# RWKV-7 time mixing: the recurrence's small products in column tiles of 32, outputs between the state products

## Chip, cores and metric

The kernel runs on one core of one Trainium2 chip. The metric is device time in microseconds (us); lower is better. A time is the median of several executions; one further execution is taken by the hardware profiler, and all rows below come from it.

## What is computed

The reference is one residual layer: RMS norm, an RWKV-7 mixer, an output projection. x is 2048 x 1024 float32, with 16 heads of 64. After projections that give r, k, v, a gate g, a decay w and a rate a for each token, each head runs a recurrence over the 2048 tokens:

```python
def step(S, inp):
    r_t, w_t, k_t, v_t, kk_t, a_t = inp
    sa = einsum('bhvk,bhk->bhv', S, -kk_t)
    S = S * w_t[:, :, None, :] + sa[..., None] * (kk_t * a_t)[:, :, None, :] + v_t[..., None] * k_t[:, :, None, :]
    y_t = einsum('bhvk,bhk->bhv', S, r_t)
    return S, y_t
```

Its output y is normalised per head and token (group norm), a bonus sum(r k r_k) v is added, the result is multiplied by silu(g) and by w_out, and x is added.

## The kernel before

**Chunks, halves, blocks.** The recurrence is computed in 64 chunks of 32 tokens (`L = 32`). The 16 heads are 8 pairs; a *wave* w is four pairs, and `h` is the head of a pair. So a chunk is two *halves*, wave 0 and wave 1, and each half issues these blocks of small products on TensorE, 64 columns of data each, in float32 (one product is two instructions in the trace, so 8 products are 16 instructions):

- **S**, `r_state` (line 245): weights `st[:, h, pair]` (128 rows x 64 columns) against the tile `x`, whose 128 rows hold the 32 tokens' values (`kv` rows), 32 rows for the results of U (`bu` rows) and the 64 x 64 state. The results of head h go to 64 PSUM rows of `bank[w]`: 32 rows for U, 32 rows with the state's part of the output. ScalarE copies the former to `misc` (line 254, two copies).
- **U**, `r_u` (line 256): the inverted 32 x 32 matrix of the chunk times these rows, 32 rows deep, in tiles of 32 x 32. ScalarE copies the result into the `bu` rows of `x` (line 265).
- **D**, `r_d` (line 267): 128 x 64 weights `dk` against `x`, into `bank[3]`; VectorE multiplies by the decay and writes the state rows of the next chunk's `x` (line 281; in the rows it has the helper's line 51).
- **Y**, `r_y` (line 284): adds to S's output rows what U's result contributes, 32 rows deep, in tiles of 32 x 32; ScalarE copies the sum to the output tile `y` (line 297).

S of a wave needs the state that D and VectorE wrote in the chunk before; U needs S's copies; D and Y need U's copies. The two waves alternate: while one waits, the other's blocks run. `chunk` (line 299) writes the order out by hand.

**Two loops.** Chunks 0 to 8 run inside the last part of the projections (`last`, `fill_last`, lines 1059 to 1171). Chunks 9 to 63 run in a loop of their own (line 1236), and three queues of other work are issued between their blocks:

- `work`: for each 128 tokens (four chunks, y tile t) a *tail* of items (`tail`, line 339), queued after chunk 4t + 4: squares on ScalarE, sums and a Newton reciprocal root on VectorE and GpSimd, normalise, gate weight and bonus on VectorE (`norm` and `bonus`, lines 407 to 414, four parts), transposes on TensorE (line 424, two groups of four, into one PSUM buffer `tps`), `shift`, `gating` and `rest` (lines 433 to 443) on VectorE with a cast on ScalarE (line 439). Chunks 12 to 40 also queue ten items of the inversions for the last two blocks of tokens (`inversion`, line 486). Each item has a nominal cost; `None` items are markers.
- `dense`: the 48 products 128 x 128 x 512 of a tail's output projection (`mm`, line 449), queued by the tail's last item.
- `evacs`: their stores.

`background(us)` (line 1193) sets its budget to `min(left + us, us)`, then issues items from `evacs` or `work` until the next one costs more than is left, or is a marker; it issues one item at least. `fill(n)` (line 328) issues dense products. `BG = 1.6` and `F = (2, 4)` are on line 29.

In a chunk, `background(BG)` is called after S of each wave (as `state`), and by `after` (line 1230) after U of each wave, there with `fill(6)`. Each engine runs its instructions in the order in which they are issued here (`manual_schedule`, line 1215).

The y tiles of this loop have three buffers. `new_y` calls `more_y` (line 1208): for t above 5 it calls `background(1)` until the second transposes of tail t - 3 have been issued.

```python
        def more_y(t):
            while t > 5 and t - 3 not in turned:
                background(1)
            return yp.tile([P, 2, NP, N], F32, name=f"y{t}", tag="y", bufs=3)
```

After the loop, line 1252 issues what is left: `while work or dense or evacs: background(2); fill(6)`.

Of the kernel before, what the change touches and what calls it, by code (L numbers as in the profile page):

```python
# [24 lines left out]
L = 32  # L25
TB = 256
NC = TB // L
NORM_EPS = 1e-6
F, BG, EV, EV0, GWE, BNE, LOW, SLOW, FAST, INV, INVC = (2, 4), 1.6, (0, 0, 0), (0, 0, 0), 0, 0, 36, 0.7, 1.3, (8, 10), 0.5
LIM = 1.0  # L30
INL = (0, 0, 3, 3, 3, 0, 0, 0)
INA, INB = (0, 0, 0, 4, 3, 3, 3, 1), (0, 0, 4, 2, 2, 2, 0, 1)
# [7 lines left out]
def rwkv7_kernel(ctx, tc, a, T):  # L40
    nc = tc.nc
# [164 lines left out]
    kv = lambda h: slice(64 * h, 64 * h + L)  # L206
    bu = lambda h: slice(64 * h + L, 64 * h + 2 * L)
    ca, cr = slice(0, L), slice(L, 2 * L)
    half = lambda h: slice(64 * h, 64 * h + 64)
    stat, dk, xs = [], [], []  # L210
# [14 lines left out]

    pls, bns, ys, misc, bank, evs, more = {}, {}, {}, [], [None] * 4, list(EV0), [None]
    first = [0]
    live = lambda w: misc[0][:, 256 * w : 256 * w + 256].rearrange("p (q n) -> p q n", q=4)

    def new_y(t):  # L230
        ys[t] = more[0](t)
# [10 lines left out]
    def ev(i, h):  # L242
        return nc.vector.tensor_copy if h < evs[i] else nc.scalar.copy

    def r_state(ch, w):
        st, x, y = stat[ch % len(stat)], xs[ch % len(xs)], bank[w][:, ch % 2]
        for p in range(4):
            for h in range(2):
                nc.tensor.matmul(y[half(h), p], st[:, h, 4 * w + p], x[:, h, 4 * w + p], start=(p == 0), stop=(p == 3),  # L249
                                 tile_position=(0, 64 * h))  # L250
        gs = live(w)
        with urgent():
            for h in range(2):
                nc.scalar.copy(gs[bu(h)], y[kv(h)])  # L254

    def r_u(ch, w):
        st, x, gs = stat[ch % len(stat)], xs[ch % len(xs)], live(w)
        for p in range(4):
            for h in range(2):
                rb = bu(h)  # L260
                nc.tensor.matmul(bank[2][rb, p], st[rb, h, 4 * w + p, ca], gs[rb, p], start=True, stop=True,
                                 tile_position=(rb.start, rb.start))
        with urgent():
            for h in range(2):
                ev(0, h)(x[bu(h), h, 4 * w : 4 * w + 4], bank[2][bu(h)])

    def r_d(ch, w):
        if ch + 1 == NCH:
            return
        d, x = dk[ch % len(dk)], xs[ch % len(xs)]  # L270
        dp = bank[3]
        for p in range(4):
            for h in range(2):
                nc.tensor.matmul(dp[half(1 - h), p], d[:, h, 4 * w + p], x[:, h, 4 * w + p], start=True, stop=True,  # L274
                                 tile_position=(0, 64 * (1 - h)))
        g, c = divmod(ch, NC)
        with urgent():
            for h in range(2):

                H = half(1 - h)  # L280
                tt(xs[(ch + 1) % len(xs)][H, h, 4 * w : 4 * w + 4], dp[H],
                   pls[g][H, c, 4 * w : 4 * w + 4, None].broadcast_to([64, 4, N]), mul)

    def r_y(ch, w):
        st, x, c = stat[ch % len(stat)], xs[ch % len(xs)], ch % 4
        for p in range(4):
            for h in range(2):
                rb = bu(h)
                nc.tensor.matmul(bank[w][rb, ch % 2, p], st[rb, h, 4 * w + p, cr], x[rb, h, 4 * w + p], start=False,  # L289
                                 stop=(p == 3), skip_group_check=True, tile_position=(rb.start, rb.start))  # L290
        t = ch // 4
        if c == 0 and w == 0:
            new_y(t)
        with urgent():
            for h in range(2):
                o = 64 * h + L * (c % 2)
                ev(2, h)(ys[t][o : o + L, c // 2, 4 * w : 4 * w + 4], bank[w][bu(h), ch % 2])

    def chunk(ch, state, fill):

        g, c = divmod(ch, NC)
        if c == 2 and g + 1 < NB:
            load_g(g + 1)
        r_state(ch, 0)
        state()
        if ch != first[0]:
            r_d(ch - 1, 1)
        fill(0)
        if ch != first[0]:
            r_y(ch - 1, 1)  # L310
        if ch + 2 < NCH:
            load_v(ch + 2)
        if ch + 3 < NCH:
            load_c(ch + 3)
        r_u(ch, 0)
        fill(1)
        r_state(ch, 1)
        state()
        r_d(ch, 0)
        fill(2)  # L320
        r_y(ch, 0)
        r_u(ch, 1)
        fill(3)

    dense, evacs, turned, served, al = deque(), deque(), set(), [0.0, 0.0], {}
    eng = lambda i: nc.gpsimd if i else nc.vector

    def fill(n):

        served[0] = min(served[0], 6) + n * (FAST if len(dense) > 2 * LOW else 1 if len(dense) > LOW else SLOW)  # L330
        while served[0] > 0 and dense:
            dense.popleft()[0]()
            served[0] -= 1
# [170 lines left out]
    with ExitStack() as p0:  # L504
# [37 lines left out]
        with ExitStack() as pa:  # L542
# [48 lines left out]
            for b in range(NB):  # L591
                (mvh, mvl), (mgh, mgl) = mixa, mixb
                lps = pps.tile([P, TB], F32, name=f"lps{b}", tag="lps", bufs=1)
                for ct in range(NCT):
                    h, dx, xt = make_h(b, ct, bc, "a")
# [3 lines left out]
                    for i in range(2):  # L599
                        tok = slice(1 - i, TB + 1 - i)  # L600
                        for k, (x, y) in enumerate(((0, hh), (0, hl), (1, hh))):
                            nc.tensor.matmul(lps, wls[i][x][:, ct], y[:, tok], start=(ct == 0 and i == 0 and k == 0),
                                             stop=(ct == NCT - 1 and i == 1 and k == 2))
# [51 lines left out]
        with ExitStack() as pb:  # L655
# [234 lines left out]
            def preload():  # L890

                misc.append(wtile("misc", [P, D], F32))
                aux = wtile("aux", [P, D], F32)
                al["gw"] = aux[:, 0:512].rearrange("p (h n) -> p h n", n=N)
                al["aux"] = iter(aux[:, x : x + 16].rearrange("p (k h) -> p k h", k=2) for x in range(512, 1024, 16))
                nc.sync.dma_start(al["gw"], a["gn_w"].rearrange("p (h n) -> p h n", n=N))
                stat.extend(wtile(f"stat{i}", [P, 2, NP, 64], F32) for i in range(4))
                dk.extend(wtile(f"dk{i}", [P, 2, NP, 64], F32) for i in range(4))
                xs.extend(wtile(f"x{i}", [P, 2, NP, N], F32) for i in range(3))
                y0 = [wtile(f"y0{t}", [P, 2, NP, N], F32) for t in range(3)]  # L900
                more[0] = lambda t: y0[t]
                for h in range(2):
                    H = half(1 - h)
                    nc.gpsimd.memset(xs[0][H, h], 0.0)

                    for x in dk:
                        nc.gpsimd.tensor_copy(x[H, h], ident[H, None, H].broadcast_to([64, NP, N]))
                load_v(0)
                load_c(0)
# [263 lines left out]
    with ExitStack() as p1:  # L1173
# [19 lines left out]
        def background(us):  # L1193

            served[1] = min(served[1] + us, us)
            fresh = True
            while evacs or work:
                u, fn = (evacs or work)[0]
                if not fresh and (u is None or u > served[1]):
                    break  # L1200
                (evacs or work).popleft()
                if u is None:
                    continue
                fresh = False
                fn()
                served[1] -= u
# [8 lines left out]
        with tc.manual_schedule(engines=MANUAL):  # L1215
            work.extend((0.7, lambda q=q: wo_split(NP - 1, q)) for q in range(2))
            for x in tail(1):
                work.extend(x)
            z = c1.tile([P, L, L], F32, name="z_")
            tm = c1.tile([P, 4 * N], F32, name="tm_")  # L1220
            inv = deque()
            for g in (NB - 2, NB - 1):
                load, *cols = inversion(g, z, lambda: tm)
                inv.extend([(0, load)] + [(None, None), (0, lambda: None)] * 4)
                inv.extend((INVC, x) for x in cols)
            inv_g = inv[L + 6][1]

            inv_last = inv[-1][1]

            def after(i):  # L1230

                if i % 2:
                    background(BG)
                    fill(sum(F))

            for ch in range(NC + 1, NCH):
                chunk(ch, lambda: background(BG), after)
                if ch % 4 == 0 and ch > NC:
                    for x in tail(ch // 4 - 1):
                        work.extend(x)  # L1240
                    for i in range(INV[1] if ch >= INV[0] else 0):
                        if inv:
                            work.append(inv.popleft())
                if ch == NCH - 2 * NC - 4:
                    assert len(inv) <= L - 1 and not any(x[1] is inv_g for x in work)
                if ch == NCH - NC - 4:
                    assert not inv and not any(x[1] is inv_last for x in work)
            r_d(NCH - 1, 1)
            r_y(NCH - 1, 1)
            for x in tail(NCH // 4 - 1):  # L1250
                work.extend(x)
            while work or dense or evacs:
                background(2)
                fill(6)
# [52 lines left out]
```

## Time and profile before

| | us |
|---|---|
| median of 3 runs (1638.33 to 1648.4) | 1640.22 |
| the profiled execution | 1642.18 |
| its span, first to last instruction | 1640.4 |

| engine | busy us | share of the span |
|---|---|---|
| TensorE, products (PE) | 1529.5 | 93% |
| TensorE, weight loads (PEld) | 1325.5 | 81% |
| VectorE (DVE) | 1192.3 | 73% |
| ScalarE (ACT) | 835.3 | 51% |
| GpSimd (POOL) | 359.8 | 22% |

The mean granted TensorE clock is 0.978 of full speed. Products are pipelined: one small product is shown with some 0.22 us, though the next starts long before its end, so a busy TensorE still has waits inside. In a row, the time in brackets is what the engine was idle before it, with what released it.

### The profile page before, as it was taken

How to read it: one execution, taken by the hardware profiler on the slowest of the kernel's cores; microseconds unless marked ns; L12 is line 12 of the kernel's file. 1: busy time of each engine (PE TensorE's matmuls, PEld its weight loads, DVE VectorE, ACT ScalarE, POOL GpSimd, SP SyncE). 2: the span in 40 equal slices, each digit the busy share in tenths (PEclk: the TensorE clock that was granted, in tenths of full speed). 3: DMA queues.
4: the chain of work that ended last, by engine and by line, in shares of the span. 5: the costliest groups of instructions: out<-in, count | busy, mean ns of one | idle time of the engine just before them, and what ended most of it. 6: DMA issues, size and time to landing. Idle time of an engine off the chain costs nothing. (4 is left out here: it accounts for less than half of the span.)

```text
span 1640.4 us, 45953 instructions
## 1 busy us (share of the span) xinstructions
PE 1529.5 (93%) x17776; PEld 1325.5 (81%) x17776; DVE 1192.3 (73%) x2844; ACT 835.3 (51%) x2126; POOL 359.8 (22%) x727
## 2 busy tenths in 40 slices
PE   3799999999989999999999999898899999999998
PEld 2589889999888888889888988777677788777776
DVE  7976776668646469797988888568568867776654
ACT  5653332233346454554545454577566666666551
POOL 4500000000002132322323232412233222323221
PEclk9899999999999999999999999799999999999999
DMA  5773433334474565666675766778866687677632
GB/s 181 225 259 126 145 117 112 127 129 155 131 233 115 124 145 139 141 155 146 156 152 153 154 160 153 216 190 236 214 186 182 176 200 207 177 182 198 177 108 81
DMA packets 445739, 269.14 MB, mean 164 GB/s; under 512 B 302768, under 2 KB 386096, under 8 KB 445520
## 3 DMA queue, kind: packets, MB, share of 16 engines
q1 hardware_dynamic: 444176, 261.67, 58.9%
q10 hardware_dynamic: 1344, 4.52, 1.0%
q8 instruction: 141, 2.31, 0.6%
q14 instruction: 78, 0.64, 0.1%
HBM read 158.74 MB, written 111.54 MB: 165 GB/s over the span
## 5 line engine op out<-in xcount | busy, mean ns | idle before, releaser
L540 PE MATMUL gps<-mixbh,wgh 128*128 128x256 f32 x512 | 147.0, 287 | 6.2 <-ACT vo L635 6.2
L540 PE MATMUL gps<-mixbl,wgh 128*128 128x256 f32 x512 | 146.5, 286 | 0.0
L540 PE MATMUL gps<-mixbh,wgl 128*128 128x256 f32 x512 | 146.4, 286 | 0.0
L254 ACT COPY misc<-ybank 32x256 f32<-32x256 f32 x220 | 79.6, 362 | 127.8 <-PE ybank L249 124.6
L540 PE MATMUL kps<-mixbl,wkh 128*128 128x256 f32 x448 | 130.4, 291 | 14.7 <-DVE mixbl L186 14.7
L51 DVE TENSOR_TENSOR x<-dp,misc 64x256 f32<-64x256 f32 x216 | 91.2, 422 | 62.7 <-PE dp L274 57.2
L846 PE MATMUL rps<-mixah,wrh 128*128 128x256 f32 x448 | 132.9, 297 | 2.1 <-ACT sq L60 2.1
L540 PE MATMUL kps<-mixbh,wkh 128*128 128x256 f32 x448 | 134.0, 299 | 0.4 <-DVE u L48 0.4
L222 POOL MEMSET x<- 32x512 f32 x128 | 66.4, 519 | 300.2 <-PE ybank L289 228.3
L540 PE MATMUL kps<-mixbh,wkl 128*128 128x256 f32 x448 | 129.3, 289 | 0.0
L846 PE MATMUL rps<-mixal,wrh 128*128 128x256 f32 x448 | 127.3, 284 | 0.0
L846 PE MATMUL rps<-mixah,wrl 128*128 128x256 f32 x448 | 127.2, 284 | 0.0
L60 ACT ACTIVATE th<-wa,dprm 128x256 f32<-128x256 f32 x64 | 30.4, 475 | 160.6 <-PE wa L798 106.2
L249 PEld LDWEIGHTS ybank<-x,stat 128*64 128x64 f32 x1760 | 64.7, 138 | 57.1 <-issue 33.5
L540 PE MATMUL vps<-wvh,mixah 128*128 128x512 f32 x256 | 104.5, 408 | 5.5 <-ACT mixah L96 4.2
L460 PE MATMUL ops<-woh,oh 128*128 128x512 f32 x256 | 107.2, 419 | 0.0
L540 PEld LDWEIGHTS gps<-mixbh,wgh 128*128 128x128 f32 x512 | 99.9, 195 | 6.9 <-ACT vo L635 6.8
L460 PE MATMUL ops<-woh,ol 128*128 128x512 f32 x256 | 105.4, 412 | 0.0
L460 PE MATMUL ops<-wol,oh 128*128 128x512 f32 x256 | 104.0, 406 | 0.0
L540 PE MATMUL vps<-wvl,mixah 128*128 128x512 f32 x256 | 101.8, 397 | 0.0
L540 PEld LDWEIGHTS kps<-mixbl,wkh 128*128 128x128 f32 x448 | 88.7, 198 | 16.0 <-DVE mixbl L186 16.0
L540 PEld LDWEIGHTS gps<-mixbl,wgh 128*128 128x128 f32 x512 | 99.9, 195 | 0.0
(325 smaller groups left out, 4575.8 us busy)
## 6 DMA issues: line engine op xcount, KB each, us to landing
stat<-sm_d SPq DMA_DIRECT2D x64, 512.0 KB, 4.8
dk<-bt_d SPq DMA_DIRECT2D x128, 128.0 KB, 4.6
sm_d<-ra SPq DMA_DIRECT2D x112, 128.0 KB, 3.2
sm_d<-mo SPq DMA_DIRECT2D x112, 128.0 KB, 2.7
bt_d<-bo SPq DMA_DIRECT2D x56, 256.0 KB, 3.3
up<-up_d SPq DMA_DIRECT2D x66, 128.0 KB, 2.6
xn<-x SPq DMA_DIRECT2D x32, 256.0 KB, 4.7
mkr_d<-mok SPq DMA_DIRECT2D x64, 128.0 KB, 1.9
```

Source lines behind the costliest of these rows:

```text
L51: return nc.vector.tensor_tensor(out=out, in0=in0, in1=in1, op=op)
L60: nc.scalar.activation(out, in_, f, **k)
L222: nc.gpsimd.memset(x[bu(h), h], 0.0)
L249: nc.tensor.matmul(y[half(h), p], st[:, h, 4 * w + p], x[:, h, 4 * w + p], start=(p == 0), stop=(p == 3), tile_position=(0, 64 * h))
L254: nc.scalar.copy(gs[bu(h)], y[kv(h)])
L460: nc.tensor.matmul(ps, l[:, ct], r(ct, ns), start=(ct == 0 and k == 0), stop=(ct == NCT - 1 and k == 2))
L540: nc.tensor.matmul(ps, x, y, start=first, stop=last)
L846: nc.tensor.matmul(ps, x, y, start=first, stop=last)
```

## The change

- S makes only the 32 columns that U needs (`ca`); each head's S result goes to 32 PSUM rows.
- Y is no longer an addition to S: `y_mm` multiplies all 128 rows of `x` with the 32 output columns (`cr`). The products of the *other* wave's output stand between S's, pair by pair, and its copies behind S's copies (`y_out`).
- U contracts all 128 rows: its operand `live` has a 128-row area for each wave and head, zero outside the `bu` rows, set to zero once.
- D makes its 64 columns as two products of 32 columns.
- All of these products are then 128 rows by 32 columns, at column 0, 32, 64 or 96.
- In the later loop `background(BG)` is called once per wave, after D, and not after U; BG is 2.4 instead of 1.6.

```diff
-F, BG, ... = (2, 4), 1.6, ...
+F, BG, ... = (2, 4), 2.4, ...
...
-    live = lambda w: misc[0][:, 256 * w : 256 * w + 256].rearrange("p (q n) -> p q n", q=4)
+    live = lambda w, h: (misc[1][:, 512:], misc[0])[w == 0][:, 256 * h : 256 * h + 256].rearrange("p (q n) -> p q n", q=4)
...
-    def r_state(ch, w):
+    def r_state(ch, w, old=None):
         st, x, y = stat[ch % len(stat)], xs[ch % len(xs)], bank[w][:, ch % 2]
         for p in range(4):
             for h in range(2):
-                nc.tensor.matmul(y[half(h), p], st[:, h, 4 * w + p], x[:, h, 4 * w + p], start=(p == 0), stop=(p == 3),
+                nc.tensor.matmul(y[kv(h), p], st[:, h, 4 * w + p, ca], x[:, h, 4 * w + p], start=True, stop=True,
                                  tile_position=(0, 64 * h))
-        gs = live(w)
+            if old:
+                y_mm(*old, p)
         with urgent():
             for h in range(2):
-                nc.scalar.copy(gs[bu(h)], y[kv(h)])
+                nc.scalar.copy(live(w, h)[bu(h)], y[kv(h)])
+        if old:
+            y_out(*old)
...
     def r_u(ch, w):
...
-                rb = bu(h)
-                nc.tensor.matmul(bank[2][rb, p], st[rb, h, 4 * w + p, ca], gs[rb, p], start=True, stop=True,
-                                 tile_position=(rb.start, rb.start))
+                nc.tensor.matmul(bank[2][bu(h), p], st[:, h, 4 * w + p, ca], live(w, h)[:, p], start=True, stop=True,
+                                 tile_position=(0, 64 * h + L))
...
     def r_d(ch, w):
...
-                nc.tensor.matmul(dp[half(1 - h), p], d[:, h, 4 * w + p], x[:, h, 4 * w + p], start=True, stop=True,
-                                 tile_position=(0, 64 * (1 - h)))
+                for o in (64 * (1 - h), 64 * (1 - h) + L):
+                    nc.tensor.matmul(dp[o : o + L, p], d[:, h, 4 * w + p, o % 64 : o % 64 + L], x[:, h, 4 * w + p], start=True,
+                                     stop=True, tile_position=(0, o))
...
-    def r_y(ch, w):
...
-                nc.tensor.matmul(bank[w][rb, ch % 2, p], st[rb, h, 4 * w + p, cr], x[rb, h, 4 * w + p], start=False,
-                                 stop=(p == 3), skip_group_check=True, tile_position=(rb.start, rb.start))
+    def y_mm(ch, w, p):
+        st, x = stat[ch % len(stat)], xs[ch % len(xs)]
+        for h in range(2):
+            nc.tensor.matmul(bank[w][bu(h), ch % 2, p], st[:, h, 4 * w + p, cr], x[:, h, 4 * w + p], start=True, stop=True,
+                             tile_position=(0, 64 * h + L))
+
+    def y_out(ch, w):
+        t, c = ch // 4, ch % 4
         if c == 0 and w == 0:
             new_y(t)
...
-    def chunk(ch, state, fill):
+    def chunk(ch, after_d, fill):
...
-        r_state(ch, 0)
-        state()
-        if ch != first[0]:
+        r_state(ch, 0, (ch - 1, 1) if go else None)
+        if go:
             r_d(ch - 1, 1)
+        after_d()
         fill(0)
-        if ch != first[0]:
-            r_y(ch - 1, 1)
...
         r_u(ch, 0)
         fill(1)
-        r_state(ch, 1)
-        state()
+        r_state(ch, 1, (ch, 0))
         r_d(ch, 0)
+        after_d()
         fill(2)
-        r_y(ch, 0)
         r_u(ch, 1)
         fill(3)
...
+                misc.append(aux)
...
+                nc.gpsimd.memset(misc[0][:, 0:512], 0.0)
+                nc.gpsimd.memset(aux[:, 512:], 0.0)
...
             def after(i):
                 if i % 2:
-                    background(BG)
                     fill(sum(F))
```

## Rows read from the trace of the kernel before

**Rows 1.** Busy time by stretch: us, then PE, PEld, DVE, ACT, POOL, clock, DMA.

```profile
1035.00:1151.50 116.50, 98.91 (x1742) 84.61 (x1743) 80.85 (x197) 79.22 (x196) 25.84 (x53) 0.93 0.78 210
1151.50:1602.30 450.80, 434.10 (x7745) 349.49 (x7746) 315.09 (x731) 277.11 (x745) 126.16 (x315) 0.98 0.68 181
1602.30:1640.40 38.10, 31.52 (x153) 25.10 (x152) 16.97 (x37) 3.86 (x10) 5.15 (x15) 0.99 0.27 83
```

**Rows 2.** State products of the later loop: ns of one, first and last start.

```profile
L249 PE MATMUL ybank<-x,stat x1760: 222/222/369, 1151.5 to 1599.4; 128*64 128x64 f32 x196
```

**Rows 3.** Timeline of TensorE, a regular half: start, us, engine, line, operation, count.

```profile
1299.29 0.69 PE L249 MATMUL ybank<-x,stat 128*64 128x64 f32 x16
1299.81 0.64 PE L274 MATMUL dp<-x,dk 128*64 128x64 f32 x16
1300.38 0.64 PE L289 MATMUL ybank<-x,stat 32*32 32x64 f32 x16
1300.85 0.67 PE L261 MATMUL ubank<-misc,stat 32*32 32x64 f32 x16
1301.44 0.50 PE L460 MATMUL ops<-woh,oh 128*128 128x512 f32 x1
...
1302.71 0.40 PE L460 MATMUL ops<-woh,ol 128*128 128x512 f32 x1
```

**Rows 4.** Timeline of TensorE, the 0.02 us from the next half's start.

```profile
1303.03 0.28 PE L249 MATMUL ybank<-x,stat 128*64 128x64 f32 x2
```

**Rows 5.** Timeline of ScalarE, the half of rows 3.

```profile
1300.08 0.75 ACT L254 COPY misc<-ybank 32x256 f32<-32x256 f32 x2 [1.24 <-PE ybank L249]
1301.09 0.74 ACT L297 COPY y<-ybank 32x256 f32<-32x256 f32 x2 [0.25 <-PE ybank L289]
1301.85 0.75 ACT L265 COPY x<-ubank 32x256 f32<-32x256 f32 x2
```

**Rows 6.** Groups of the later loop: busy us, mean ns of one, idle before.

```profile
L51 DVE TENSOR_TENSOR x<-dp,misc 64x256 f32<-64x256 f32 x216 | 91.2, 422 | 62.7 <-PE dp L274 57.2
L460 PE MATMUL ops<-woh,oh 128*128 128x512 f32 x214 | 90.9, 425 | 0.0
L249 PE MATMUL ybank<-x,stat 128*64 128x64 f32 x1760 | 81.5, 229 | 14.6 <-DVE x L51 7.9 <-ACT sq L60 2.8 <-DMA v<-v_d 2.4
L51 DVE TENSOR_TENSOR y<-y,rst 128x256 f32<-128x256 f32 x56 | 32.6, 582 | 23.1 <-POOL rst L383 23.1
L410 DVE TENSOR_TENSOR y<-y,aux 128x256 f32<-128x256 f32 x56 | 32.5, 580 | 1.9
L414 DVE TENSOR_TENSOR y<-y,v 128x256 f32<-128x256 f32 x56 | 25.4, 453 | 5.6 <-POOL v L362 2.7
L51 DVE TENSOR_TENSOR ol<-gt,oh 128x512 fp32r<-128x512 f32 x29 | 19.9, 685 | 13.2 <-ACT oh L439 12.4
L439 ACT CAST oh<-gt 128x512 fp32r<-128x512 f32 x28 | 17.3, 619 | 3.3 <-DVE gt L51 2.9
```

**Rows 7.** Timeline of TensorE, transposes ahead of a D block.

```profile
1439.49 0.66 PE L424 MATMUL yt<-consts,y 128*128 128x128 f32 x4
1440.08 0.69 PE L274 MATMUL dp<-x,dk 128*64 128x64 f32 x16
```

**Rows 8.** Timeline of TensorE, the half that starts at 1587.44.

```profile
1587.44 1.04 PE L249 MATMUL ybank<-x,stat 128*64 128x64 f32 x15 [2.04 <-DVE x L51]
...
1590.23 1.06 PE L261 MATMUL ubank<-misc,stat 32*32 32x64 f32 x16
1591.22 0.80 PE L460 MATMUL ops<-woh,oh 128*128 128x512 f32 x1
```

**Rows 9.** Busy time by stretch, that half: columns as in rows 1.

```profile
1587.00:1594.00 7.00, 6.50 (x70) 5.15 (x70) 4.49 (x12) 2.18 (x6) 0.00 (x0) 0.59 0.24 76
```

**Rows 10.** Timeline of VectorE behind the loop, from shift to last remainder.

```profile
1618.89 0.69 DVE L51 TENSOR_TENSOR yt<-yt,prm 128x512 f32<-128x512 f32 x1
...
1623.75 0.69 DVE L51 TENSOR_TENSOR ol<-gt,oh 128x512 fp32r<-128x512 f32 x1 [0.69 <-ACT oh L439]
```

More of the change, by code (lines that the diff above doesn't have):

```diff
@@ L28 @@
 NORM_EPS = 1e-6
-F, BG, EV, EV0, GWE, BNE, LOW, SLOW, FAST, INV, INVC = (2, 4), 1.6, (0, 0, 0), (0, 0, 0), 0, 0, 36, 0.7, 1.3, (8, 10), 0.5
+F, BG, EV, EV0, GWE, BNE, LOW, SLOW, FAST, INV, INVC = (2, 4), 2.4, (0, 0, 0), (0, 0, 0), 0, 0, 36, 0.7, 1.3, (8, 10), 0.5
 LIM = 1.0
@@ L248, in r_state @@
             for h in range(2):
-                nc.tensor.matmul(y[half(h), p], st[:, h, 4 * w + p], x[:, h, 4 * w + p], start=(p == 0), stop=(p == 3),
+                nc.tensor.matmul(y[kv(h), p], st[:, h, 4 * w + p, ca], x[:, h, 4 * w + p], start=True, stop=True,
                                  tile_position=(0, 64 * h))
-        gs = live(w)
+            if old:
+                y_mm(*old, p)
         with urgent():
             for h in range(2):
-                nc.scalar.copy(gs[bu(h)], y[kv(h)])
+                nc.scalar.copy(live(w, h)[bu(h)], y[kv(h)])
+        if old:
+            y_out(*old)
     def r_u(ch, w):
-        st, x, gs = stat[ch % len(stat)], xs[ch % len(xs)], live(w)
+        st, x = stat[ch % len(stat)], xs[ch % len(xs)]
         for p in range(4):
             for h in range(2):
-                rb = bu(h)
-                nc.tensor.matmul(bank[2][rb, p], st[rb, h, 4 * w + p, ca], gs[rb, p], start=True, stop=True,
-                                 tile_position=(rb.start, rb.start))
+                nc.tensor.matmul(bank[2][bu(h), p], st[:, h, 4 * w + p, ca], live(w, h)[:, p], start=True, stop=True,
+                                 tile_position=(0, 64 * h + L))
         with urgent():
@@ L282, in r_d @@
                    pls[g][H, c, 4 * w : 4 * w + 4, None].broadcast_to([64, 4, N]), mul)
-    def r_y(ch, w):
[L285 to L288, printed above, removed]
-                nc.tensor.matmul(bank[w][rb, ch % 2, p], st[rb, h, 4 * w + p, cr], x[rb, h, 4 * w + p], start=False,
-                                 stop=(p == 3), skip_group_check=True, tile_position=(rb.start, rb.start))
-        t = ch // 4
+    def y_mm(ch, w, p):
+        st, x = stat[ch % len(stat)], xs[ch % len(xs)]
+        for h in range(2):
[3 more added lines that the diff above has]
+        t, c = ch // 4, ch % 4
         if c == 0 and w == 0:
@@ L297, in r_y @@
                 ev(2, h)(ys[t][o : o + L, c // 2, 4 * w : 4 * w + 4], bank[w][bu(h), ch % 2])
-    def chunk(ch, state, fill):
+    def r_y(ch, w):
+        for p in range(4):
+            y_mm(ch, w, p)
+        y_out(ch, w)
+    def chunk(ch, after_d, fill):
         g, c = divmod(ch, NC)
+        go = ch != first[0]
         if c == 2 and g + 1 < NB:
             load_g(g + 1)
-        r_state(ch, 0)
-        state()
-        if ch != first[0]:
+        r_state(ch, 0, (ch - 1, 1) if go else None)
+        if go:
             r_d(ch - 1, 1)
+        after_d()
         fill(0)
-        if ch != first[0]:
-            r_y(ch - 1, 1)
         if ch + 2 < NCH:
@@ L894, in preload @@
                 al["gw"] = aux[:, 0:512].rearrange("p (h n) -> p h n", n=N)
-                al["aux"] = iter(aux[:, x : x + 16].rearrange("p (k h) -> p k h", k=2) for x in range(512, 1024, 16))
+                misc.append(aux)
+                al["aux"] = iter(misc[0][:, x : x + 16].rearrange("p (k h) -> p k h", k=2) for x in range(736, 1024, 16))
+                nc.gpsimd.memset(misc[0][:, 0:512], 0.0)
+                nc.gpsimd.memset(aux[:, 512:], 0.0)
                 nc.sync.dma_start(al["gw"], a["gn_w"].rearrange("p (h n) -> p h n", n=N))
```

## The prediction

> **What bounds the kernel now.** I read the busy time by stretch first, then the timeline of one regular half of the later loop, then the groups of that loop. The later loop (chunks 9 to 63, two halves each) takes 450.8 of the 1640.4 us, and TensorE is busy for 434 of them, VectorE for 315, ScalarE for 277 [rows 1]. Its 110 state blocks start between 1151.5 and 1599.4, so a half lasts 4.1 us on average [rows 2]. A regular one lasts 3.74, from 1299.29 to 1303.03: S at 0, D at 0.52, Y at 1.09, U at 1.56, six dense products from 2.15, the next S [rows 3, 4]. So a half is 2.15 us plus 0.265 for each dense product (1.59 / 6).
>
> Why U starts at 1.56 decides what this change can win. Y ends its issue just then, so TensorE looks like the bound. But U multiplies what ScalarE copies from S, and these copies run from 1300.08 to 1300.83; U starts at 1300.85 [rows 3, 5]. U could not start earlier even if Y were not there.
>
> Above the regular halves stand, in this loop: 110 x 2.15 + 640 dense products x 0.265 = 406 us (three groups of 213 or 214 [rows 6]); 28 groups of transposes at up to 0.59, the time from such a group to the D block behind it [rows 7], 16 us; waits of S, 14.6 us [rows 6]; some 14 us are left for the lower clock and small waits.
>
> **The blocks, part by part.** S now makes 32 columns per head instead of 64, and Y's products (32 columns, 128 rows deep) stand between S's. Contracting 128 rows instead of 32 costs nothing that I can see: Y with 32 rows takes 0.47, S with 128 rows 0.52 [rows 3]. Each block has 16 instructions, as each product is two. In the first 0.02 us of a block two products start [rows 4], and the block issues in about 0.47 (0.69 less the 0.22 of the last one [rows 2, 3]): two column tiles run side by side, eight rounds of 0.06. The new S+Y block has 32 instructions on four column tiles. If four run side by side it also takes eight rounds, 0.47; if only two do, 0.94. No row has four. I take 0.47, as the starts within a round are under 0.02 us apart while a round lasts 0.06, so there is room for two more. D becomes 32 instructions on four tiles: 0.47 against 0.94 likewise. U keeps 16 on two tiles. So Y's block goes, S+Y, D and U stay.
>
> The gain on the path is nothing. S's last result comes when it did, its copies end 1.54 us after S starts, U starts at 1.56, and TensorE idles where Y was (from about 1.0). The half stays at 2.15 + 0.265 n. What uses the hole are the transposes, now issued there: up to 16 us less. Y's copies now come right behind S's on ScalarE, before the tails' work; nothing waits for them.
>
> The Trainium skill, "TensorEngine Tiling (Array Packing)", Key Properties, says that a change of tiling mode drains TensorE. The trace agrees: the step to a block in another mode is 0.57 to 0.59, without a change 0.47 to 0.52 [rows 3]. By that rule alone one change less per half would give 110 x 0.1 = 11 us; by the copies in rows 5 it gives none, since U waits for them.
>
> S+Y gains a wait: Y's operand is U's result, copied by ScalarE, and everything later on TensorE queues behind it. In a regular half these copies end at 1302.60, 0.4 ahead of S [rows 5]. Where a gate's cast stands ahead of them on ScalarE, the cover is gone (below). The two memsets that zero the padded operand are a microsecond or so on GpSimd in the stage before: nothing.
>
> **The tails' queue.** This decides. Tail work (normalise, gate, transpose) and the inversions go through background(), which issues queued items until a budget of nominal costs is used, and stops at each None marker whatever is left. Before: four calls per chunk with 1.6. After: two with 2.4. A tail comes every four chunks, so it now has 8 calls. Walking its items by the rule: (squares, reductions, scale) (wait) (wait, norm and bonus 0) (norms and bonuses 1, 2) (norm, bonus 3) (transpose 0) (shift, gate 0) (transpose 1) (rest, shift, gate) (rest, dense): about ten calls, and two to three more for the inversions' ten items and the stores. Ten to thirteen calls do not fit into 8. Before, 16 did.
>
> The queue therefore grows until new_y (line 1209) needs a y buffer: from chunk 24 on, the first output of every fourth chunk must first issue the tail three before up to its second transpose, in calls of 1.0. Walking the queue by the nominal costs gives 7, 10, 8, 7, 14, 10, 10, 10, 3 and 3 forced calls at chunks 24, 28, ... 60, and leaves 50 items at the loop's end, where the old schedule leaves 3.
>
> Price of ten forced calls, issued between S+Y and D of one half: VectorE first does three norm parts at 0.58 + 0.58 + 0.45, 4.8 us, then shift and gate, 0.69 each [rows 6]; the second transpose reuses the PSUM tile that the gate reads, so it and D, behind it on TensorE, start only then: 6.2 + 0.6 [rows 7] = 6.8 after S, instead of 0.5. D is 6.3 late. Then the next S+Y waits: D's products 0.8, two multiplies 0.88, rest, shift and gate 2.1 on VectorE, the cast 0.62 and U's copies 0.75 behind it on ScalarE [rows 5, 6]: 5.2 us after D's start, while TensorE has U and four dense products, 2.1 us. Another 3.1. Together 9.4. The burst of 14 has one norm part and two waits more, about 13; those of 7 or 8 about 8; those of 3 only the second wait and little else, 4. Sum: 4 x 9.4 + 13 + 3 x 8 + 2 x 4 = 83 us.
>
> The clock adds to that. After an idle 2.04 us at 1587 the granted clock of the stretch was 0.59, a mixture of the two levels 2.4 and 1.2 GHz [rows 8, 9], and U with its change of mode took 0.99 instead of 0.59 [rows 3, 8]; a half at that rate is 2.5 us longer. Eight large bursts leave TensorE idle twice as long, 3 to 4 us: 8 x 2.5 = 20. (Bounds: 0 if it stays up, 40 with two falls per burst.)
>
> Loop after: 110 x 2.15 + 587 dense products x 0.265 = 392 (one tail and five products fewer in the loop), bursts 83, clock 20, waits of S as now 15: 510 against 450.8, **+59**.
>
> **Behind the loop.** Now 38.1 us [rows 1]: one tail's chain and its dense products. After, a third of tail 13 and all of tail 14 stand ahead of tail 15 on VectorE. From shift to the last remainder took 5.5 us (1618.89 to 1624.44) [rows 10]; a tail's norms and six 0.69 operations are 10.5 [rows 6], and up to 20 with its waits. That is 16 to 25 more; the 85 extra dense products (about 20 us) fit into those waits. I take **+22**.
>
> **Chunks 0 to 8.** TensorE is busy for 98.9 of 116.5 us [rows 1]. 17 Y blocks of 0.47 are 8 us at most, none where U waits for ScalarE, and a late U copy can cost a little: -8 to +4, I take **-4**.
>
> Sum: the profiled execution took 1642.2, 2 above the median 1640.2. 1642.2 + 59 + 22 - 4 = 1719, as a median **1717**.
>
> **Rivals.** *Four column tiles don't run side by side.* For it: no row has more than two. Against: the close starts [rows 4]. S+Y then takes 0.94, S's copies and U come 0.47 later in each half: 110 x 0.47 = 52, so 1769. In the same direction the Trainium skill, "TensorE: Matmul & The Clock Gate", section "Wait — 56ns, not 53.3ns?", says that starts never come less than about 25 ns apart. Two starts within 0.02 us [rows 4] speak against it at first sight; by that figure a block of 32 would be an estimated 0.80, and the time 1753.
>
> *The bursts cost nothing and the kernel is faster.* The forced items are work that VectorE must do anyway, and it is busy only 70% of the loop; the multiplies behind D now stand ahead of the tails' work. If VectorE has run ahead and the transposes find their inputs, only 392 + 15 of the loop remain: 1640.2 - 44 + 22 - 4 = 1614. Against it: norm to second transpose is one chain on one engine. It decides where bursts and clock together cost under 26 us, 2.6 per burst instead of 10.
>
> *Bursts at about half price*, with VectorE one or two norm parts ahead and no fall of the clock: 1717 - 40 - 20 = 1657 at the least.
>
> **Chances.** Forecast 0.65 (1670 to 1750: clock 0 or 40, bursts a third off); four tiles 0.15; half price 0.1; faster 0.1. The range 1650 to 1785 leaves out the faster case and a little at the top. A measurement here tells about 1% (16 us) from no change: faster 0.1, within 1% 0.05, slower 0.85.
>
> **What would show it.** Right: S+Y with 32 starts in 0.47 and D too; U still 1.55 after S; idle where Y was; from chunk 24, every eighth half, two groups of transposes in a row between S+Y and D with D about 6 us late; 55 to 60 us behind the last U. Wrong: regular halves of 4.2 (tiles), or under 3.5 (the copies don't bind U); no halves of 8 to 10 us (queue).

## The result and the profile after

The changed kernel took 1710.38 us (median of 4 runs, 1703.95 to 1715.29), the kernel before 1642.17 beside it (4 runs, 1638.33 to 1648.4): a ratio of 1.0403, interval 1.0377 to 1.0429. The forecast was slower, 1717 us in 1650 to 1785. The profiled execution spans 1710.1 us, 69.7 more than before.

First the busy time by stretch, columns as in [rows 1]: the stretch ahead of the later loop, the loop to its last U, and what is behind it.

```profile
1035.00:1145.30 110.30, 90.36 (x2031) 77.11 (x2032) 80.66 (x197) 79.12 (x196) 24.59 (x53) 0.92 0.83 223
1145.30:1645.00 499.70, 423.39 (x9403) 307.84 (x9403) 281.87 (x698) 273.27 (x738) 119.15 (x300) 0.92 0.58 159
1645.00:1710.10 65.10, 50.12 (x223) 38.02 (x221) 33.56 (x70) 6.93 (x16) 10.29 (x30) 0.95 0.28 83
```

Against [rows 1] the loop starts 6.2 us earlier (1145.3 for 1151.5), lasts 48.9 longer (499.7 for 450.8), and 27.0 more stand behind it (65.1 for 38.1). VectorE did less in the longer loop (282 us for 315): work that the loop used to do is done behind it.

A regular half has not become longer. This is the timeline of TensorE and ScalarE in one, to be read beside [rows 3, 5]:

```profile
1259.21 0.25 PE L254 MATMUL ybank<-x,stat 128*32 128x64 f32 x2
1259.23 0.25 PE L296 MATMUL ybank<-x,stat 128*32 128x64 f32 x2
...
1259.64 0.23 PE L296 MATMUL ybank<-x,stat 128*32 128x64 f32 x2
1259.68 0.63 PE L283 MATMUL dp<-x,dk 128*32 128x64 f32 x32
1259.96 0.75 ACT L260 COPY misc<-ybank 32x256 f32<-32x256 f32 x2 [0.96 <-PE ybank L296]
1260.37 1.02 PE L269 MATMUL ubank<-misc,stat 128*32 128x64 f32 x16
...
1261.32 0.50 PE L472 MATMUL ops<-woh,oh 128*128 128x512 f32 x1
```

S (L254) and Y (L296) start in pairs 0.01 to 0.02 us apart, and the last of 32 instructions starts 0.43 after the first, so four column tiles do run side by side. D starts at 0.47. S's copies run from 0.75 to 1.50 after S. U begins at 1.16, when the first of the two is done, and stretches over the second: its busy time is 1.02 us where [rows 3] show 0.67. Dense products start at 2.11 after S, before at 2.15. The half is 3.70, before 3.74 [rows 3, 4]. (3.70 is also the median of all halves here; before it was 3.90, as the queue's work stood in more of them.)

The loss is in the forced bursts. Timeline of TensorE, VectorE and ScalarE in the one at chunk 48, whose S starts at 1503.81:

```profile
1504.40 0.85 PE L436 MATMUL yt<-consts,y 128*128 128x128 f32 x4
...
1507.25 0.69 DVE L51 TENSOR_TENSOR yt<-yt,prm 128x512 f32<-128x512 f32 x1
1507.98 0.69 DVE L51 TENSOR_TENSOR gt<-yt,gt 128x512 f32<-128x512 f32 x1
1508.82 0.63 PE L436 MATMUL yt<-consts,y 128*128 128x128 f32 x4 [3.57 <-DVE gt L51]
1509.38 0.81 PE L283 MATMUL dp<-x,dk 128*32 128x64 f32 x32
1510.23 0.88 DVE L51 TENSOR_TENSOR x<-dp,misc 64x256 f32<-64x256 f32 x2 [1.56 <-PE dp L283]
...
1513.08 0.62 ACT L451 CAST oh<-gt 128x512 fp32r<-128x512 f32 x1 [2.86 <-DVE gt L51]
1513.72 0.75 ACT L273 COPY x<-ubank 32x256 f32<-32x256 f32 x2
1514.14 0.30 PE L296 MATMUL ybank<-x,stat 128*32 128x64 f32 x2 [0.79 <-ACT x L273]
```

The second transposes wait 3.57 us for the gate that frees their tile; D is behind them, 5.57 us after S instead of 0.47. The next gate's cast then stands ahead of U's copies on ScalarE, so the next half's Y starts at 1514.14, 4.76 after D. Waits of TensorE in the loop (what waited, for what; us in total, times, longest):

```profile
PE yt L436 <- DVE gt L51: 28.4, 8, 3.7
PE ybank L296 <- ACT x L273: 19.9, 16, 2.5
```

And on the page, the costliest groups, VectorE's wait for D:

```profile
L51 DVE TENSOR_TENSOR x<-dp,misc 64x256 f32<-64x256 f32 x216 | 91.2, 422 | 201.1 <-PE dp L283 197.0
```

It was 62.7 [rows 6]. VectorE works less and waits more, and it waits for the engine that waits for it: the two hold each other up.

### The profile page after: what moved, and what is told of

Its sections match the earlier page's. It is cut to its first block, busy times and chain, and to the rows that moved or that the text cites. A ratio compares the mean times of both kernels' runs of the same rounds, so it can differ in the third digit from the quotient of the medians.

```text
span 1710.1 us, 49898 instructions
## 1 busy us (share of the span) xinstructions
PE 1527.9 (89%) x19792; PEld 1287.5 (75%) x19792; DVE 1175.1 (69%) x2844; ACT 835.6 (49%) x2126; POOL 357.9 (21%) x729
## 4 chain that ended last, share of the span: by engine, by line
PE 49%; DVE 23%; ACT 9%; DMA 7%; issue 4%; SPq 1%; POOL 1%; DVEq 0%; ACTq 0%; POOLq 0%
PE gps L552 10%; PE ops L472 8%; PE kps L552 7%; PE rps L858 6%; PE vps L552 3%; PE ubank L269 3%; PE ybank L254 2%; PE mps L894 2%; DVE z L51 2%; ACT aux L260 2%; DVE tm L51 2%; PE ybank L296 2%; DVE x L51 1%; ACT misc L260 1%; PE dp L283 1%
## 5 line engine op out<-in xcount | busy, mean ns | idle before, releaser
L472 PE MATMUL ops<-woh,oh 128*128 128x512 f32 x256 | 111.0, 434 | 3.4 <-ACT oh L451 3.4
L472 PE MATMUL ops<-woh,ol 128*128 128x512 f32 x256 | 111.2, 434 | 0.0
L552 PEld LDWEIGHTS gps<-mixbh,wgl 128*128 128x128 f32 x512 | 99.4, 194 | 0.0
L296 PE MATMUL ybank<-x,stat 128*32 128x64 f32 x1760 | 79.7, 226 | 22.0 <-ACT x L273 19.9
```

The lines of the kernel that those rows point to most:

```text
L296: nc.tensor.matmul(bank[w][bu(h), ch % 2, p], st[:, h, 4 * w + p, cr], x[:, h, 4 * w + p], start=True, stop=True, tile_position=(0, 64 * h ...
L472: nc.tensor.matmul(ps, l[:, ct], r(ct, ns), start=(ct == 0 and k == 0), stop=(ct == NCT - 1 and k == 2))
L552: nc.tensor.matmul(ps, x, y, start=first, stop=last)
```

## The experiments

A row's line numbers are those of the kernel that ran. Every ratio is to the kernel before, with its 95% interval.

**The blocks or the calls?** First the changed blocks with the old calls: the call after S instead of D, and again one after U.

```diff
-F, BG, ... = (2, 4), 2.4, ...
+F, BG, ... = (2, 4), 1.6, ...
...
         r_state(ch, 1, (ch, 0))
-        r_d(ch, 0)
         after_d()
+        r_d(ch, 0)
...
                 if i % 2:
+                    background(BG)
                     fill(sum(F))
```

> The new blocks with the queue calls of the kernel before: four calls a chunk (after S and after U of each wave), BG 1.6. Queue theory: no forced call, some 3 items left behind the loop, no half with two transposes in a row ahead of D. The time is that of the kernel before less the 6 us that chunks 0 to 8 won (they last 1145 instead of 1151 us in the changed kernel): 1625 to 1645. Rival, the blocks themselves cost the time (four column tiles, the zero-padded operand, Y's wait inside S): the time stays above 1680.

Measured: 1634.77 us, ratio 0.9952 (0.9936 to 0.9968). Next the kernel before with the new calls: one of 2.4 after D, none after U.

```diff
-F, BG, ... = (2, 4), 1.6, ...
+F, BG, ... = (2, 4), 2.4, ...
...
         r_state(ch, 1)
-        state()
         r_d(ch, 0)
+        state()
...
                 if i % 2:
-                    background(BG)
                     fill(sum(F))
```

> The old blocks with the queue calls of the changed kernel: two calls a chunk, after D, BG 2.4, none after U. Queue theory: forced calls from chunk 24 on (walked: 4, 10, 8, 6, 14, 10, 10, 10, 3, 3), now ahead of Y's copies, some 53 items left, 60 to 65 us behind the loop, 1700 to 1745. Rival, the blocks cost it: 1640 to 1650.

Measured: 1774.37 us, ratio 1.0807 (1.0775 to 1.084). The calls alone cost 8% in the old order of blocks and 4.5% in the new one (1.0403 for 0.9952); the blocks alone bring half a per cent. I had expected less of the second run (1700 to 1745). Why it loses more is in its timeline around the burst at chunk 44 (S at 1498.91), and in its busy time by stretch at chunk 28, one half per row:

```profile
1507.61 1.09 PE L424 MATMUL yt<-consts,y 128*128 128x128 f32 x4 [3.31 <-DVE gt L51]
1508.63 1.06 PE L261 MATMUL ubank<-misc,stat 32*32 32x64 f32 x16
...
1517.17 0.74 ACT L297 COPY y<-ybank 32x256 f32<-32x256 f32 x2
...
1517.96 0.48 PE L249 MATMUL ybank<-x,stat 128*64 128x64 f32 x4 [2.10 <-ACT y L297]
```

```profile
1316.88:1330.00 13.12, 7.00 (x78) 4.92 (x77) 6.88 (x16) 2.84 (x8) 1.90 (x4) 0.72 0.45 126
1330.00:1336.34 6.34, 4.58 (x69) 3.84 (x69) 2.74 (x5) 2.10 (x6) 1.04 (x2) 0.77 0.33 106
1336.34:1342.95 6.61, 6.61 (x70) 5.29 (x70) 3.77 (x9) 2.88 (x8) 0.00 (x0) 0.50 0.55 119
```

There the forced calls come out of Y, behind D, so D is on time, but U, the copies behind it and the next half stand behind the transposes. A third half is drawn in too, which waits for an output copy behind a cast, or runs whole at the lower level, 1.2 GHz (granted clock 0.50). Over these three halves the ten bursts cost 134 us (their sum less three of 3.74); in the changed kernel 84.7 in two.

Does the place of the first call matter? The changed blocks, a call of 1.6 after D and one after U:

```diff
-F, BG, ... = (2, 4), 2.4, ...
+F, BG, ... = (2, 4), 1.6, ...
...
                 if i % 2:
+                    background(BG)
                     fill(sum(F))
```

> The changed kernel with a call after U put back, so four calls a chunk (after D and after U), BG 1.6. Queue theory: no forced call, about 38 us behind the loop, 1630 to 1650. If the place of the call (after D instead of after S) were what costs, it stays near 1700.

Measured: 1633.17 us, ratio 0.9948 (0.9919 to 0.9977). It doesn't.

**Number of calls or budget?** The changed kernel with two calls of 1.2 where it has one of 2.4, then with one call of 4.8:

```diff
-                chunk(ch, lambda: background(BG), after)
+                chunk(ch, lambda: (background(1.2), background(1.2)), after)
```

> The changed kernel with two background calls behind D instead of one, each with half the budget (1.2), so 16 calls per tail and the same nominal 2.4 per half. My theory (the forced calls at new_y set the time, at about 1.0 us each, 84.7 us for 82 calls; both markers and budget limit the queue): walking the queue gives 59 forced calls, none at chunks 24 and 28, and 50 items left behind the loop: the loop 415 + 61 = 476, behind it 65, so 1675 to 1700. Rival (the number of calls alone was the fault): no forced calls, 1620 to 1640.

Measured: 1675.93 us, ratio 1.0204 (1.0177 to 1.023); profiled span 1673.0, of which the loop 466.4 and behind it 65.8. No burst at chunks 24 and 28, as the walk said; the six large ones at 32 to 52 cost 7.2, 7.9, 5.8, 6.1, 7.1 and 7.1 us (two halves less 7.4). More calls alone don't do it: they win back half of the loss (1.0204 for 1.0403), and the rival, 1620 to 1640, is out. The forced calls came out cheaper than the 1.0 us each of my theory: all ten bursts cost 42 us for the 59 calls of the walk.

```diff
-F, BG, ... = (2, 4), 2.4, ...
+F, BG, ... = (2, 4), 4.8, ...
```

> The changed kernel with its single call per half behind D, but a budget of 4.8 instead of 2.4. My theory: markers hold the queue back whatever the budget, but less is forced: walking it gives 24 forced calls in place of 82, in bursts of 1 to 6, and 48 items left behind the loop: the loop 415 + 25 = 440, behind it 62, so 1635 to 1660. Rival one (the number of calls alone decides): as the changed kernel, 1700 to 1715. Rival two (the budget alone decides): no forced calls and about 40 us behind the loop, 1615 to 1630.

Measured: 1696.96 us, ratio 1.0326 (1.0302 to 1.0351). More than I expected. Few calls are forced, but a call of 4.8 is a burst itself. Its timeline of ScalarE, TensorE and VectorE in the two halves of chunk 29, where no call is forced:

```profile
1321.44 0.62 ACT L451 CAST oh<-gt 128x512 fp32r<-128x512 f32 x1 [1.83 <-DVE gt L51]
1322.09 0.75 ACT L273 COPY x<-ubank 32x256 f32<-32x256 f32 x2
...
1322.50 0.63 PE L296 MATMUL ybank<-x,stat 128*32 128x64 f32 x3 [1.69 <-ACT x L273]
...
1327.07 0.65 PE L283 MATMUL dp<-x,dk 128*32 128x64 f32 x29
...
1332.40 0.38 DVE L51 TENSOR_TENSOR z__15783<-z__15783,tm__15784 128x210 f32<-128x210 f32 x1
1332.81 0.88 DVE L51 TENSOR_TENSOR x<-dp,misc 64x256 f32<-64x256 f32 x2
```

In the first a tail's gate and cast, issued in one go, stand ahead of U's copies, and Y waits for them. In the second D's results wait 5 us for their multiplies, behind columns of the inversion (`z_`), and so does the next S. Over the loop, TensorE's wait for U's copies alone is longer than in the changed kernel (19.9):

```profile
PE ybank L296 <- ACT x L273: 26.8, 20, 2.5
```

So the price is of queued work issued in a lump, forced or not; counting forced calls gives the time only while the regular calls stay small.

**The clock.** The forecast put 20 us on the lower clock behind the bursts. To price it, D's products were issued eight times more behind the first transposes of each forced burst, so that TensorE doesn't idle there (D itself overwrites the result):

```diff
         def more_y(t):
             while t > 5 and t - 3 not in turned:
+                was = t - 2.5 in turned
                 background(1)
+                if t - 2.5 in turned and not was:
+                    r_d(4 * t, 0, 9)
```

(`r_d(ch, w, 9)` issues eight sets of products and no multiplies; the first transposes of a tail put its `t - 2.5` into `turned`.)

> The changed kernel, and in each forced burst, right behind the first transposes, D's products eight times more (their result is overwritten by D itself): about 3.3 us of work for TensorE in the 3.6 us in which it waits for the gate. It separates the clock's price from the waiting. As forecast the clock costs 20 us: 1690. By the changed kernel's trace (D 0.77 instead of 0.41, U and the next half's blocks likewise, most of it inside waits) it is under 1 us a burst: 1702 to 1711. Right for either: D behind the burst issues in about 0.41.

Measured: 1733.75 us, ratio 1.0536 (1.0502 to 1.0569), outside both forecasts. Inconclusive: the 256 instructions took 5 to 8 us, longer than the hole of 3.6, and D came 7.7 to 10.8 us after S (15.2 at chunk 40). With three sets (96 instructions; the 4 in the call makes three, not the four of the expectation):

```diff
-                    r_d(4 * t, 0, 9)
+                    r_d(4 * t, 0, 4)
```

> The changed kernel with D's products issued four times more (128 instructions whose result D itself overwrites) behind the first transposes of each forced burst, half as many as in the run before that kept TensorE warm, so that they fit into the 3.6 us in which it idles there. The forecast put the lower clock behind the bursts at 20 us beside bursts of 83. If the clock costs that much by itself: 1685 to 1695. If it lies inside the bursts' waits, as their measured 84.7 us including the clock suggest: 1703 to 1715.

Measured: 1707.45 us, ratio 1.0381 (1.0348 to 1.0413), no different from the changed kernel's 1.0403. The busy time by stretch shows how, at chunk 44 from the burst's S to the next half's Y and from there to the next S, the changed kernel first, then this run:

```profile
1465.66:1477.08 11.42, 6.54 (x97) 4.62 (x96) 7.66 (x17) 3.07 (x8) 0.52 (x1) 0.70 0.44 134
1477.08:1481.52 4.44, 4.26 (x84) 3.09 (x84) 2.73 (x7) 2.52 (x7) 1.03 (x2) 1.00 0.51 133
```

```profile
1466.77:1477.18 10.41, 5.96 (x193) 4.45 (x192) 7.53 (x16) 3.08 (x8) 0.53 (x2) 1.00 0.58 162
1477.18:1482.65 5.47, 5.38 (x84) 4.29 (x85) 2.93 (x7) 2.53 (x7) 1.04 (x2) 0.69 0.49 143
```

At full clock (a granted 1.00, the level of 2.4 GHz, where it was 0.70) the first stretch is 1.0 us shorter. But now the clock is low behind it (0.69, where it was 1.00), and the second stretch is 1.0 longer: 15.9 stays 15.9. The same run's timeline at chunk 48, its S at 1504.96, shows what holds most of the first stretch:

```profile
1509.14 0.69 DVE L51 TENSOR_TENSOR gt<-yt,gt 128x512 f32<-128x512 f32 x1
1509.97 0.63 PE L445 MATMUL yt<-consts,y 128*128 128x128 f32 x4 [2.09 <-DVE gt L51]
...
1514.10 0.62 ACT L460 CAST oh<-gt 128x512 fp32r<-128x512 f32 x1 [2.71 <-DVE gt L51]
1514.74 0.75 ACT L273 COPY x<-ubank 32x256 f32<-32x256 f32 x2
1515.16 0.70 PE L304 MATMUL ybank<-x,stat 128*32 128x64 f32 x3 [2.17 <-ACT x L273]
```

Here the second transposes start 5.01 after S, in the changed kernel 5.01 too (1508.82); Y starts 10.20 after S, there 10.33. The chain runs over VectorE and ScalarE, and a faster TensorE waits for it: 0.13 us for a granted clock of 1.00 instead of 0.83 there. Over the eight large bursts the pairs of halves sum to 73.5 us here and 76.3 in the changed kernel (each less 7.4): 2.8 us, between 0.7 lost and 2.3 gained in one.

Most of the time at the lower level does lie inside waits: by the granted clock, the ten pairs spend 72 us at 1.2 GHz in the changed kernel and 44 here, and these 28 us less make them 3.3 shorter. But that is not the clock's whole price, as the run also moved the lower level. Behind Y the granted clock is 0.66 to 0.73 in seven of the eight bursts here, and in five in the changed kernel. Where only one of the two has it there (chunks 40, 44, 48 and 52), that stretch is 0.8 to 1.1 us longer. Ahead of Y the clock rose at six chunks (28 to 48), which saved 4.7 us together. From these I estimate 4.7 + 5 x 1.0, about 10 us, for the lower clock in the changed kernel's eight large bursts. No run shows the time with the clock up in both stretches of all of them.

**The tile that ties transposes to the gate.** Two PSUM tiles for the transposes; to find room, U's and D's results share one:

```diff
-        sps, tps = pool("sps", 1, space=PSUM), pool("tps", 1, space=PSUM)
+        sps, tps = pool("sps", 1, space=PSUM), pool("tps", 2, space=PSUM)
...
-        bank[2] = sps.tile([P, 4, N], F32, name="ubank")
-        bank[3] = sps.tile([P, 4, N], F32, name="dp")
+        both = sps.tile([P, 2, 4, N], F32, name="both")
+        bank[2], bank[3] = both[:, 0], both[:, 1]
```

> The changed kernel with two PSUM buffers for the transposes (U's and D's results share a bank to make room), so that the second transposes no longer wait for the gate that reads the first. Theory, D is held by the chain norm 3 - shift - gate - second transposes: D in the large bursts comes 1.4 us earlier (4.2 instead of 5.6 after S at the burst near 1504) and eight bursts give 8 to 14 us: 1696 to 1703. Rival, the norms alone hold VectorE and the multiplies behind D: no change within 4 us.

Measured: 1753.72 us, ratio 1.0673 (1.0631 to 1.0714). In the large bursts D came 3.0 to 3.7 us after S instead of 5.6 to 6.6 (10.4 instead of 13.0 at chunk 40), so the tile does hold D there. But the edit did something I had not foreseen, in every regular half. Timeline of TensorE, VectorE and ScalarE in one (S at 1253.98):

```profile
1254.72 0.75 ACT L260 COPY misc<-ybank 32x256 f32<-32x256 f32 x2 [1.48 <-PE ybank L296]
1255.25 0.86 DVE L51 TENSOR_TENSOR x<-both,misc 64x256 f32<-64x256 f32 x2 [2.92 <-PE both L283]
1255.49 0.74 ACT L306 COPY y<-ybank 32x256 f32<-32x256 f32 x2
1256.25 0.64 PE L269 MATMUL both<-misc,stat 128*32 128x64 f32 x16 [1.17 <-ACT y L306]
```

U's input is there at 1255.47, yet U starts at 1256.25, 2.27 after S instead of 1.16. Two things have just ended: VectorE's multiplies of D's results (1256.11), which now read the tile that U writes, and ScalarE's output copies, to which the profile puts the wait. Other halves tell them apart. In the burst at chunk 28:

```profile
1337.40 0.86 DVE L51 TENSOR_TENSOR x<-both,misc 64x256 f32<-64x256 f32 x2
1338.05 0.74 ACT L306 COPY y<-ybank 32x256 f32<-32x256 f32 x2
1338.41 0.90 PE L269 MATMUL both<-aux,stat 128*32 128x64 f32 x14 [1.29 <-DVE x L51]
```

U starts 0.15 us after the end of the multiplies (1338.26) and 0.38 ahead of the end of the copies (1338.79). In 107 of 108 halves of the loop the step from the multiplies' end to U is 0.14 or 0.15 us (in one 0.42), while that from the copies' end goes from -0.38 to 0.60: U waits for the multiplies. The Trainium skill, "PSUM — Partial Sum Buffer", section "PSUM bank collisions raise a hardware error", tells of a compiler's scheduler that adds a dependency between any two instructions on different engines that touch the same bank in the same 32 partitions, reads and writes alike; the trace agrees with such an order, though no run here shows whether the bank or the shared tile brings it in. The half is 4.41 instead of 3.70, 110 x 0.71 = 78 us, while the loop is only 42.7 longer (542.4): the ten bursts cost 60 (two halves less 8.82) instead of 84.7, and the rest came back in other halves. As a test of the time it failed.

**Better calls.** The changed blocks with 1.2 after D and 2.0 after U:

```diff
-F, BG, ... = (2, 4), 2.4, ...
+F, BG, ... = (2, 4), 1.2, ...
...
                 if i % 2:
+                    background(2.0)
                     fill(sum(F))
```

> As the last one, but calls of 1.2 after D and 2.0 after U, the same 6.4 per chunk. The call after D issues work that ScalarE does ahead of U's copies, which S+Y now waits for; the call after U issues behind them. Queue theory: no forced call; less of the wait in S+Y, so 5 to 15 us below the last one: 1620 to 1640. Rival, the split of the budget doesn't matter: the same as the last one.

Measured: 1624.58 us, ratio 0.9894 (0.9866 to 0.9922): faster than both kernels, the fastest found, and 8.6 us below the version with 1.6 and 1.6. The expected reason is a small part of that: Y's wait for U's copies is 0.4 us over the loop, and was only 2.6 there. The loop and what is behind it:

```profile
1146.90:1574.80 427.90, 394.91 (x9432) 288.46 (x9433) 301.41 (x712) 275.79 (x742) 123.31 (x310) 1.00 0.70 189
1574.80:1624.60 49.80, 40.10 (x194) 31.63 (x192) 27.35 (x56) 4.89 (x12) 8.06 (x21) 0.99 0.26 78
```

The stretch behind the loop is 12 us longer than in [rows 1]. So the obvious next step was 2.4 after U, to leave nothing behind:

```diff
-                    background(2.0)
+                    background(2.4)
```

> New blocks with a call of 1.2 behind D and one of 2.4 behind U (the best version so far had 1.2 and 2.0; it left 20 items behind the loop, which then lasted 49.8 us, though its loop was 20 us shorter than that of the version with 1.6 and 1.6). Walking the queue gives no forced call and 2 items left. My theory: the loop stays at 428 to 436 and the stretch behind it falls to about 39: 1612 to 1624. Rival (the shorter loop of 1.2 and 2.0 came from work left undone): the loop is as with 1.6 and 1.6, 445 to 449, and the time 1628 to 1636.

Measured: 1644.43 us, ratio 0.9997 (0.9975 to 1.0019).

```profile
1141.60:1597.80 456.20, 413.65 (x9493) 301.83 (x9493) 316.52 (x732) 278.06 (x745) 126.52 (x315) 0.99 0.66 179
1597.80:1634.20 36.40, 29.79 (x134) 23.86 (x132) 16.96 (x37) 3.32 (x8) 5.16 (x15) 1.00 0.27 83
```

Behind the loop 13.4 us are gone, and the loop is 28.3 longer, in an execution of 1636.22 us, one of the fastest of ten. My theory failed and the rival came nearer, with 7 us more in the loop than it allows. Its reason covers only a part: 37 more dense products in the loop (645 for 608) are some 10 us at 0.265 each. And 26 halves last over 4.65 us, where the other version has 8. In one of them (chunk 44, S at 1433.56) the cast of a gate that the larger call issued stands ahead of S's copies on ScalarE (1434.26 to 1434.88), so U starts 1.76 after S instead of 1.16; and eight dense products stand behind U, as `fill(6)` issues more than six where that queue is long. How much is the work and how much the larger call wasn't told apart.

**The hole where Y was.** TensorE idles from the end of D to U. In the version with 1.2 and 2.0, two of the six dense products moved there:

```diff
                 if i % 2:
                     background(2.0)
-                    fill(sum(F))
+                fill(F[i % 2])
```

> The run with calls of 1.2 and 2.0, and two of the six dense products of a half now stand between D and U, four behind U. Theory, U waits for ScalarE's copies of S and TensorE has a hole of about 0.6 us there: the regular half falls from 3.70 to 3.25 to 3.35, as in the halves with transposes there; VectorE (70% busy) then holds back some of it: 1585 to 1612. Rival, TensorE's issue is the bound and the hole is not real: 1620 to 1640.

Measured: 1625.24 us, ratio 0.9893 (0.985 to 0.9936), the same as without. The time is the rival's, but not for its reason: the hole is real, as regular halves did fall from 3.70 to 3.39, but only 22 of the 110 are such. Waits of TensorE in the loop, first with the six together, then with two in the hole:

```profile
PE ybank L254 <- DVE x L51: 5.0, 9, 0.9
PE ybank L254 <- POOL x L222: 2.1, 3, 1.0
```

```profile
PE ybank L254 <- DVE x L51: 11.0, 13, 1.9
PE ybank L254 <- POOL x L222: 9.2, 6, 3.2
```

S now waits 13 us longer for VectorE's multiplies and for GpSimd's writes to `x`; the loop is 430.7, for 427.9. The same edit in the kernel before, where Y fills the hole:

```diff
                 if i % 2:
                     background(BG)
-                    fill(sum(F))
+                fill(F[i % 2])
```

> The kernel before with the same split, two dense products between D and Y, four behind U. There Y fills the time until the copies end, so nothing is won: U comes 0.5 us later and the half stays 3.74 or grows by the two more changes of mode, about 0.1 to 0.3 us: 1640 to 1675. If the copies did not bind U in the kernel before, it would be the same as before.

Measured: 1658.39 us, ratio 1.0087 (1.0056 to 1.0118), as expected: without a hole, it only delays U (2.22 after S instead of 1.55, medians of all halves).

## Why the prediction was right, point by point

- *The blocks bring nothing on the path.* Right: a regular half is 3.70 for 3.74, and the blocks alone are worth 0.5%. The reason was right too (S's copies bind U), though not its detail: I put U at 1.55 after both copies; it starts at 1.16 after the first, stretches over the second and ends when I said. That transposes in the hole bring up to 16 us is not borne out: with calls of 1.6 behind D and U the loop is 448.9, for 450.8 before, though those of the call behind D stand in the hole. The rule of drains at a change of tiling mode (the Trainium skill, "TensorEngine Tiling (Array Packing)", Key Properties) would have made it 11 us; the blocks alone took 8 us off the whole time, of which 3.3 in the loop (447.5 for 450.8 in the profiles).
- *Four column tiles run side by side.* Right: 32 instructions start in 0.43 us, 0.014 each. The estimate of 1753 from at least 25 ns between starts (the Trainium skill, "TensorE: Matmul & The Clock Gate", section "Wait — 56ns, not 53.3ns?") falls with it: that figure doesn't hold between column tiles here.
- *The queue decides.* Right, and shown by undoing the calls alone. Bursts stood at the ten chunks of the walk; those of three forced calls cost 4.1 and 4.2 (forecast 4), that of 14 calls 14.6 (13), those of 7 or 8 9.9, 9.1 and 8.2 (8), those of ten 9.0, 8.5, 7.4 and 9.7 (9.4).
- *D 6.8 after S in a burst.* 5.57 at chunk 48, up to 6.6 in the other large ones (13.0 at chunk 40). At chunk 48 VectorE reached the shift 3.4 us after S (1507.25), not 4.8: eight norm operations stood between, not nine, and they took 0.42 each, where I had taken the loop's means of 0.45 to 0.58 [rows 6]. Y came 4.76 after D, forecast 5.2.
- *The clock, 20 us, beside bursts of 83.* These two terms were mis-sized together: all ten bursts cost 84.7 us with the clock in it, 18 less than I added up. The clock does fall (0.70 at chunk 44, above), but by the estimate above it is worth about 10 us in the eight large bursts: 0.1 to 1.0 us ahead of Y, where most of the stretch is a chain over VectorE and ScalarE, and some 1.0 behind it, not 2.5 per burst. The rest of the 18 lies in the waits: D came 0.2 to 1.2 us earlier than forecast in seven of the eight.
- *The rest.* The loop without its bursts is 415.0 (499.7 less 84.7), forecast 392 + 15; behind it +27.0, forecast 22; chunks 0 to 8 -6.2, forecast -4. The loop's +48.9 for +59 is 18 too many for bursts and clock against 8 too few for the rest. With 5 too few behind the loop and 2 too many ahead of it, the whole sum is 7 us off, less than its parts: that closeness is luck.

## What to carry to other kernels

When work is fed into a tight loop by a budget, count what one call can issue (its stops as well as its budget) against what arrives, before judging the instructions that were changed: here the changed products were worth 0.5% and the two dropped calls 4.5 to 8%. Work that misses its turn does not just come late, it comes in one lump, in front of everything behind it on every engine. And a stall's price is mainly the length of the chain that sets its end. A slower clock inside it is in part paid for already: price it where it shows, behind the stall too, before adding it to the sum. Keeping TensorE busy inside the stall returned nothing that the time shows here.

## What the runs showed of the hardware that I had not expected

- 32 instructions (16 products) with 128 x 32 weights on four column tiles start in 0.43 us, a pair of S and one of Y 0.01 to 0.02 apart; the 16 instructions of the former S on two tiles took 0.47. Doubling the tiles doubled the rate.
- Two results in one PSUM tile made U start 1.1 us later in every regular half, 0.14 or 0.15 us after VectorE had read the other result, though U writes other columns.
- 96 further instructions in the idle time kept the granted clock at 1.00 up to the next half's Y at chunk 44, where it was 0.70; behind that Y it was 0.69, where it had been 1.00.
